# The last four adaLN vectors moved to the tensor engine, and longer pauses between the parts of the recurrences

## The chip, the cores and the metric

One Trainium2 chip, of which the kernel uses one core. The metric is the device time of one execution in microseconds (us); the figure for the kernel before is the median of three runs.

## The reference

One layer of an encoder trunk on `x` (1024 positions x 1024 channels) with a conditioning vector `c` (1024). Everything is float32.

```python
cond = silu(c)
mod = cond @ w_ada + b_ada                       # 1024 x 6144
sh1, sc1, gt1, sh2, sc2, gt2 = split(mod, 6)
h = rms_norm(x, g_pre_mix) * (1 + sc1) + sh1
u, v, rg_g, rg_x, ft_x = split(h @ w_in)         # 256, 256, 512, 512, 256 columns
y_gm = spatial_gating(gelu(u), gelu(v))
xr = centred_depthwise_conv(rg_x)
y_rg = bidirectional_rg_lru(xr) * gelu(rg_g)     # gates, then one scan per direction
y_ft = fourier_mix(ft_x)                         # real part of a 2-D DFT, then a linear map
y = concat(rms_norm(y_gm), rms_norm(y_rg), rms_norm(y_ft))
x = x + gt1 * rms_norm(y @ w_out, g_post_mix)
h = rms_norm(x, g_pre_ff) * (1 + sc2) + sh2
x = x + gt2 * rms_norm(square(relu(h @ w_ff1)) @ w_ff2, g_post_ff)
```

The change is about `mod`: `sh1` and `sc1` are needed at once, but `gt1`, `sh2`, `sc2` and `gt2` (the late vectors) only after the output projection `y @ w_out`.

## The kernel before

Channels lie on the partitions and positions along the free axis. `h` is kept in `HL` as a high and a low fp32r part; each large product is three fp32r matmuls (high by high, low by high, high by low: `mm3`, line 149). A 512-column matmul of this kind makes half of the positions of one 128-channel tile.

The part of the kernel around the change runs so:

- **zk**: the product of `h` with the 768 columns of `w_in` for the recurrence (tiles 0 to 3) and the Fourier group (tiles 4 and 5), first half of the positions for all, then the second half (line 672).
- **rg** (line 497), in a task `rg_all`: for each of four channel tiles a convolution (`conv`, DVE), two directions of gate matmuls (`gz`, 12 each), tanh, exp and square root on ACT, multiplications and a scan on DVE. The `yield`s in lines 526, 531 and 540 say how much matmul time shall pass before the next part is put into the program. The sum of the two directions is on POOL (line 541).
- **Fourier**: `ft_fold` (line 587) folds a tile by symmetry on POOL; `ft_a` (`fa`, `fx`) and `ft_b` (`fe`) are fp32 matmuls. `SEQ` (line 23) says in which order folds (f), first steps (a), second steps (b) and tiles of the remaining input projection (z) are written.
- **z tiles** 0, 1, 4, 5 (`z_full`), then `v_mm` (`vp`), then z tiles 6 and 7 in halves, with the layer norm of v, the spatial mixing (`rw`, `sp`) and three group norms (`gss`, `grs`, `dg`) between them, and then the output projection (`op`). From the start of `op` to the end, 741 us, the kernel computes what the change leaves alone.
- **ada** (line 452): for each of the 32 late blocks of 128 outputs, a 512 KB load of 128x1024 weights and one DVE instruction that multiplies by `cond`, which is spread over all partitions, and sums along the row. The task starts after the recurrences have ended (`join(trg)`, then `spawn(ada_all())`, line 710).

What sets the order: `mm` (line 142) adds each matmul's columns to a clock of the program; `pump` steps the tasks that are due by it. On each engine the instructions then stand in a fixed order and run strictly in that order. All loads are issued by SP, in order too. `load` takes one of four buffers of the tag "r", so a load waits until the last reader of the buffer's earlier content is done; the weights of `w_in`, `w_v`, `w_out` and the gates use the same four. For w_in and w_v the last reader is the instruction that makes the low part, on POOL (`WE`, line 171).

Of the kernel before, what the change touches and what calls it, by code (L numbers as in the profile page):

```python
# [7 lines left out]
F32 = mybir.dt.float32  # L8
# [11 lines left out]
PF = 7  # L20
CG = 8
RS = ((4.1, 2.0, 3.1, 2.1, 4.2), (3.1, 2.0, 2.6, 1.1, 3.7), (2.6, 2.0, 2.6, 0.6, 0.7))
SEQ = 'f0 f1 z02 a0 a1 b0 b1 z12 z42 z52'
WE = 'GGGGGGGG'
GD = ('VV VV VV VV', 'VV VV', 'V V V V')
FW = (3.5, 4.5, 1.5)
# [5 lines left out]
OEs = ('VV', 'VV', 'GG')  # L32
NG = (2.0, 5.0)
NR = ((4.5, 3.0), (8.0, 2.0))
ADY = (1.6, 32, 3)
RH = (2, 3)
D = 1024
S = 1024
# [5 lines left out]
_n = 0  # L44
for _name, _w in (("b_ada", 48), ("g_pre_mix", 8), ("g_post_mix", 8), ("g_pre_ff", 8), ("g_post_ff", 8),
                  ("g_mix_out", 8), ("conv_w", 16), ("conv_b", 4), ("b_a", 8), ("b_x", 8), ("lam", 8),
                  ("ft_b", 2), ("ln_g", 2), ("ln_b", 2)):
    PV[_name] = (_n, _w)
    _n += _w
NPV = _n  # L50


@with_exitstack
def trunk(ctx, tc, xT, c, pv, ident, w_ada, w_k, w_in, w_v, gates, k1, k2, k3, gmft, w_out, w_ff1, w_ff2, out):
    nc = tc.nc
    const = ctx.enter_context(tc.tile_pool(name="const", bufs=1))
    pool = ctx.enter_context(tc.tile_pool(name="pool", bufs=21))
# [19 lines left out]
    def ctile(name, n, dt=F32, bufs=1):  # L77
        return const.tile([128, n], dt, name=name, tag=name, bufs=bufs)
# [6 lines left out]
    ab = ctile("ab", 56)  # L85
    sp = ctile("sp", 64)

    ctile("pad0", 8)
    HL = const.tile([128, 8, 2, 1024], F32R, name="HL", tag="HL")
    big = const.tile([128, 8, 1024], F32, name="big", tag="big")  # L90
    ctile("pad1", 8)
    a1, b1, a2, b2, g1, g2, bp1 = (ab[:, i * 8:i * 8 + 8] for i in range(7))

    def col(name, i, n=1):
        a = PV[name][0] + i
        return pvt[:, a:a + n]
# [3 lines left out]
    clock = [0.0]  # L100
# [351 lines left out]
    def ada(blk):
        r = load(w_ada[blk], tag="r")
        V.scalar_tensor_tensor(out=r, in0=r, scalar=0.5, in1=cond, op0=MUL, op1=MUL,  # L454
                               accum_out=mod[:, blk:blk + 1])

    def vec(dst, blk, gname, one):
        V.tensor_tensor(out=dst, in0=mod[:, blk:blk + 8], in1=col("b_ada", blk, 8), op=ADD)
        if one:
            V.tensor_scalar(out=dst, in0=dst, scalar1=1.0, scalar2=None, op0=ADD)  # L460
        if gname:
            V.tensor_tensor(out=dst, in0=dst, in1=col(gname, 0, 8), op=MUL)

    def ada_all():
        for blk in range(16, 48):
            ada(blk)
            yield ADY[0] if blk < ADY[1] else ADY[2]
        vec(g1, 16, "g_post_mix", False)
        vec(b2, 24, None, False)
        vec(a2, 32, "g_pre_ff", True)  # L470
        vec(g2, 40, "g_post_ff", False)
# [25 lines left out]
    def rg(t):  # L497
        gs = gs_t.pop(t)
        xh, xl = xs_t.pop(t)
        xr = xr_t.pop(t)  # L500
        st = []
        for d in range(2):
            i = d * 4 + t
            ti, av = big[:, 2 + t, :] if d == 0 else tt("ti"), tt("av")
            pp = []
            for j in range(2):
                o = (d * 2 + j) * 128
                p = pa("gz")
                mm3(p, gs[:, o:o + 128], gs[:, 512 + o:640 + o],
                    [(xh[:, a:b], xl[:, a:b]) for a, b in HALF], True, True)  # L510
                pp.append(p)
                yield 0.1
            rr = [th("rr"), th("rr")] if t in RH else pp[0]
            for h, (a, b) in enumerate(HALF):
                A.activation(out=rr[h], in_=pp[0][h], func=AF.Tanh, scale=0.5, bias=bah[:, i:i + 1])
            for h, (a, b) in enumerate(HALF):
                A.activation(out=ti[:, a:b], in_=pp[1][h], func=AF.Tanh, scale=0.5, bias=bxh[:, i:i + 1])
            for h, (a, b) in enumerate(HALF):
                A.activation(out=av[:, a:b], in_=rr[h], func=AF.Exp, scale=m4[:, i:i + 1], bias=m4[:, i:i + 1])  # L519
            for h, (a, b) in enumerate(HALF):  # L520
                last = A.activation(out=rr[h], in_=rr[h], func=AF.Tanh, scale=p2[:, i:i + 1],
                                    bias=p2[:, i:i + 1])
            V.scalar_tensor_tensor(out=ti, in0=ti, scalar=1.0, in1=xr, op0=ADD, op1=MUL)
            V.scalar_tensor_tensor(out=ti, in0=av, scalar=1.0, in1=ti, op0=ADD, op1=MUL)
            st.append((rr, ti, av))
            yield 2.5
        with tc.issue_after(last.ins):
            for d in range(2):
                for h in range(2):
                    rgl[0] = A.activation(out=st[d][0][h], in_=st[d][0][h], func=AF.Sqrt, scale=0.25).ins  # L530
        yield 1.0
        for d in range(2):
            sq, ti, av = st[d]
            for h, (a, b) in enumerate(HALF):
                V.tensor_tensor(out=ti[:, a:b], in0=ti[:, a:b], in1=sq[h], op=MUL)
            if d == 0:
                V.tensor_tensor_scan(ti, av, ti, 0.0, op0=MUL, op1=ADD)  # L537
            else:
                V.tensor_tensor_scan(ti[:, ::-1], av[:, ::-1], ti[:, ::-1], 0.0, op0=MUL, op1=ADD)
            yield 1.2  # L540
        G.tensor_tensor(out=st[0][1], in0=st[0][1], in1=st[1][1], op=ADD)

    def norm_group(ks, n):
# [85 lines left out]

    def ft_b(t, at, ax):  # L630
        cosE = [kt[1][:, i * 257:i * 257 + 257] for i in range(3)]
        sinE = [kt[2][:, i * 257:i * 257 + 257] for i in range(2)]
        cosO = [kt[3][:, i * 256:i * 256 + 256] for i in range(2)]
        sinO = [kt[3][:, 512 + i * 256:768 + i * 256] for i in range(2)]
        ba = [at[:, j * 128:j * 128 + 128] for j in range(8)]
        ps = [pb("fe") for _ in range(4)]
        Ec, Es, Oc, Os = ps[0][:, 0:257], ps[1][:, 0:257], ps[2][:, 0:256], ps[3][:, 0:256]
        for dst, pairs in ((Es, ((ba[4], sinE[0]), (ba[5], sinE[1]))),
                           (Ec, ((ba[0], cosE[0]), (ba[1], cosE[1]), (ax, cosE[2]))),
                           (Os, ((ba[6], sinO[0]), (ba[7], sinO[1]))),  # L640
                           (Oc, ((ba[2], cosO[0]), (ba[3], cosO[1])))):
            for j, (w, x) in enumerate(pairs):
                mm(dst, w, x, j == 0, j == len(pairs) - 1)
            pump()
        y = big[:, 6 + t, :]
        b = col("ft_b", t)
        sn = [th("sn", F32, 257), th("sn", F32, 256)]
        A.copy(sn[0], Es)
        A.copy(sn[1], Os)
        Es, Os = sn  # L650
        V.scalar_tensor_tensor(out=y[:, 0:513:2], in0=Ec, scalar=b, in1=Es, op0=ADD, op1=SUB)
        V.scalar_tensor_tensor(out=y[:, 514:1024:2], in0=Ec[:, 255:0:-1], scalar=b, in1=Es[:, 255:0:-1], op0=ADD, op1=ADD)
        V.scalar_tensor_tensor(out=y[:, 1:512:2], in0=Oc, scalar=b, in1=Os, op0=ADD, op1=SUB)
        V.scalar_tensor_tensor(out=y[:, 513:1024:2], in0=Oc[:, ::-1], scalar=b, in1=Os[:, ::-1], op0=ADD, op1=ADD)

# [16 lines left out]
    for m in range(2, 6):  # L672
        p = {m: pb("zk")}
        for k in range(8):
            stage_mm(k, 1, p, (m,))
        evac_z(m, p, 1, V if m % 2 else A)
        if m == 2:
            kt[2] = load(k2, 770, "k2", "t")
            gm = load(gmft, 1024, "gm", "t")
        if m == 3:  # L680
            prep_to(1)
            for i, src, n in ((1, k1, 771), (3, k3, 1024)):
                kt[i] = load(src, n, "k%d" % i, "t")
# [23 lines left out]
            z_full(t, int(q[2]))  # L707
    kt.clear()
    join(trg)
    tad = spawn(ada_all(), 0.0)  # L710
    with tc.issue_after(rgl[0]):
        for t in range(2):
            A.activation(out=big[:, t, :], in_=big[:, t, :], func=AF.Gelu_apprx_tanh)
# [651 lines left out]
def _layout(inp):  # L1365
# [7 lines left out]
        cols(f("g_post_ff")[0]), cols(f("g_mix_out")[0]), cols(f("rg_conv_w")[0].reshape(-1)),  # L1373
        cols(f("rg_conv_b")[0]), cols(f("rg_b_a")[0].reshape(-1)), cols(f("rg_b_x")[0].reshape(-1)),
        cols(f("rg_lam")[0].reshape(-1)), cols(f("ft_b")[0].reshape(-1)), cols(f("gm_ln_g")[0]),
        cols(f("gm_ln_b")[0])], axis=1)
    w_in = f("w_in")[0]
    wi = w_in.reshape(8, 128, 14, 128).transpose(2, 1, 0, 3).reshape(14, 128, 1024)[:8]
    wv = w_in[:, 256:512].reshape(2, 4, 128, 256).transpose(0, 2, 1, 3).reshape(2, 128, 1024)
# [23 lines left out]
    for e in range(2):  # L1403
# [47 lines left out]
```

## Time and profile before

| | |
|---|---|
| median of three runs | 1030.87 us (1029.47 to 1032.01) |
| profiled execution | 1031.33 us, span 1029.5 us |
| PE busy | 963.3 us (94%) |
| DVE busy | 766.4 us (74%) |
| ACT busy | 501.0 us (49%) |
| POOL busy | 123.8 us (12%) |
| zk second half, rg, Fourier, first z tiles | about 90 to 214 us |
| vp, z tiles 6 and 7, norms | 214 to 288 us |
| op and feed-forward | 288 us to the end |

A time in the trace is counted from the start of the span. PE busy is the time in which a matmul was under way, at whichever clock; the granted clock (PEclk, 1.00 is full speed) stands beside it. Idle time of PE between two matmuls is put down to what the second one waited for.

### The profile page before, as it was taken

The page shows a single profiled execution, that of the slowest core. Times are in us where ns is not written, and L with a number is a line of the kernel's source. Part 1 is how long each engine was busy: PE and PEld are TensorE (multiplying, and loading weights), DVE is VectorE, ACT ScalarE, POOL GpSimd, SP SyncE. Part 2 cuts the span into 40 slices and gives each one's busy share as a digit, 9 for nine tenths or more (in the row PEclk, how much of TensorE's full clock was granted, in tenths as well). Part 3 has the DMA queues.
Part 4 walks back from the last instruction along what each step waited for, and adds up shares of the span by engine and source line. Part 5 has one row for each costly group of instructions (what it writes and reads, how often), then busy time and mean ns, then how long its engine had stood idle before and what let it go on. Part 6 is the DMA issues. An engine that isn't in the chain of part 4 may idle for free.

```text
span 1029.5 us, 13104 instructions
## 1 busy us (share of the span) xinstructions
PE 963.3 (94%) x4756; PEld 804.0 (78%) x4756; DVE 766.4 (74%) x1059; ACT 501.0 (49%) x764; POOL 123.8 (12%) x82
## 2 busy tenths in 40 slices
PE   6789975997899999999999999999999999999995
PEld 2568854896677997988888888888888888888995
DVE  6978888778897678897776776757665777688464
ACT  4454876622454355564544544545444455446311
POOL 4400391321140341000000000000000000000000
PEclk7989987998899999999999999999999999999998
DMA  9740200158235323054343343359899979987532
GB/s 343 286 142 21 82 24 18 62 202 288 102 131 177 129 97 113 32 183 185 132 179 138 133 191 126 123 198 331 297 392 341 362 269 335 328 277 258 187 133 93
DMA packets 80003, 191.59 MB, mean 186 GB/s; under 512 B 8769, under 2 KB 13121, under 8 KB 77890
## 3 DMA queue, kind: packets, MB, share of 16 engines
q1 hardware_dynamic: 76482, 186.56, 50.7%
q10 hardware_dynamic: 3456, 4.20, 1.1%
q8 instruction: 37, 0.61, 0.2%
q14 instruction: 28, 0.23, 0.1%
HBM read 144.58 MB, written 46.14 MB: 185 GB/s over the span
## 4 chain that ended last, share of the span: by engine, by line
PE 73%; DVE 14%; DMA 4%; ACT 4%; issue 3%; POOL 1%; SPq 0%; DVEq 0%; POOLq 0%
PE f L143 59%; PE op L143 6%; DMA raw<-in_w_ada_dram 3%; DVE raw L454 2%; PE z L143 2%; PE zk L143 2%; PE grs L143 1%; PE r L143 1%; DVE raw L291 1%; DVE HL L325 1%; DVE xr L481 1%; DVE big L537 1%; DMA big<-in_xT_dram 1%; ACT av L519 1%; DVE ss L279 1%
## 5 line engine op out<-in xcount | busy, mean ns | idle before, releaser
L143 PE MATMUL f<-x,x 128*128 128x512 f32 x768 | 236.2, 389 | 0.0
L143 PEld LDWEIGHTS f<-x,x 128*128 128x128 f32 x768 | 144.1, 188 | 29.8
L143 PE MATMUL f<-HL,wc 128*128 128x512 f32 x672 | 158.1, 390 | 0.0
L937 ACT CAST x<-R 128x1024 fp32r<-128x1024 f32 x96 | 100.3, 1053 | 110.8 <-DVE R L1131 56.0
L143 PE MATMUL f<-x 128*128 128x512 f32 x384 | 149.4, 389 | 0.0
L143 PEld LDWEIGHTS f<-HL,wc 128*128 128x128 f32 x672 | 125.0, 188 | 28.2 <-ACT big L1067 2.3
L948 DVE TENSOR_TENSOR x<-R,x 128x1024 fp32r<-128x1024 f32 x96 | 116.7, 1221 | 32.1 <-ACT x L937 30.7
L143 PE MATMUL f<-hc,wc 128*128 128x512 f32 x504 | 118.8, 389 | 0.0
L143 PEld LDWEIGHTS f<-hc,wc 128*128 128x128 f32 x504 | 94.6, 188 | 19.7
L143 PE MATMUL op<-HL,hi 128*128 128x256 f32 (+1 forms) x384 | 88.4, 324 | 0.0
L143 PEld LDWEIGHTS f<-x 128*128 128x128 f32 x384 | 72.1, 188 | 15.1
L143 PEld LDWEIGHTS op<-HL,hi 128*128 128x128 f32 x384 | 64.3, 190 | 6.5 <-issue 1.4
L1131 DVE TENSOR_TENSOR R<-R,o 128x512 f32<-128x512 f32 x64 | 43.6, 688 | 33.3 <-DMA o<-in_w_ff_dram 23.9
L143 PE MATMUL z<-HL,hi 128*128 128x512 f32 x192 | 63.3, 433 | 0.7 <-ACT ftg L614 0.7
L171 POOL TENSOR_TENSOR lo<-raw,hi 128x1024 fp32r<-128x1024 f32 x16 | 44.3, 2775 | 155.7 <-ACT hi L170 111.0
L143 PE MATMUL op<-HL,lo 128*128 128x256 f32 (+1 forms) x192 | 61.5, 320 | 0.0
L937 ACT CAST wc<-S 128x1024 fp32r<-128x1024 f32 x28 | 29.5, 1053 | 60.0 <-DVE S L1042 56.4
L454 DVE SCALAR_TENSOR_TENSOR raw<-raw,cond 128x1024 f32<-128x1024 f32 x32 | 48.5, 1521 | 13.4 <-DMA raw<-in_w_ada_dram 13.2
L948 DVE TENSOR_TENSOR wc<-S,wc 128x1024 fp32r<-128x1024 f32 x28 | 34.2, 1222 | 21.6 <-PE f L143 20.0
L143 PEld LDWEIGHTS z<-HL,hi 128*128 128x128 f32 x192 | 38.5, 204 | 11.9 <-issue 3.7
L143 PE MATMUL f<-HL,w 128*128 128x256 f32 x384 | 47.6, 285 | 0.0
L143 PEld LDWEIGHTS f<-HL,w 128*128 128x128 f32 x384 | 46.6, 192 | 0.6 <-issue 0.5
(298 smaller groups left out, 1637.8 us busy)
## 6 DMA issues: line engine op xcount, KB each, us to landing
raw<-in_w_ada_dram SPq DMA_DIRECT2D x48, 512.0 KB, 4.9
R<-Y SPq DMA_DIRECT2D x96, 256.0 KB, 4.8
R<-in_w_ff_dram SPq DMA_DIRECT2D x80, 256.0 KB, 5.0
raw<-in_w_ff_dram SPq DMA_DIRECT2D x32, 512.0 KB, 3.3
Y<-big SPq DMA_DIRECT2D x16, 1024.0 KB, 3.9
o<-in_w_ff_dram SPq DMA_DIRECT2D x64, 256.0 KB, 5.1
Y<-big SPq DMA_DIRECT2D x13, 768.0 KB, 3.4
SS<-R SPq DMA_DIRECT2D x32, 256.0 KB, 5.0
```

The lines of the kernel that those rows point to most:

```text
L143: pe[0] = T.matmul(o, w, x, start=start, stop=stop, skip_group_check=more).ins
L171: (eng or V).tensor_tensor(out=lo, in0=src, in1=hi, op=SUB)
L279: ssl[0] = eng.tensor_tensor(out=ss, in0=ss, in1=sq, op=ADD).ins
L291: V.scalar_tensor_tensor(out=r1, in0=r1, scalar=0.5, in1=cond, op0=MUL, op1=MUL, accum_out=mod[:, 8 + k:9 + k])
L325: V.scalar_tensor_tensor(out=HL[:, k, 1, a:b], in0=xk, scalar=b1[:, k:k + 1], in1=HL[:, k, 0, a:b], op0=ADD, op1=SUB)
L454: V.scalar_tensor_tensor(out=r, in0=r, scalar=0.5, in1=cond, op0=MUL, op1=MUL, accum_out=mod[:, blk:blk + 1])
L481: V.scalar_tensor_tensor(out=xr[:, o0:o1], in0=z[:, i0:i1], scalar=col("conv_w", k * 4 + t), in1=xr[:, o0:o1], op0=MUL, op1=ADD)
L519: A.activation(out=av[:, a:b], in_=rr[h], func=AF.Exp, scale=m4[:, i:i + 1], bias=m4[:, i:i + 1])
L537: V.tensor_tensor_scan(ti, av, ti, 0.0, op0=MUL, op1=ADD)
L937: order[0] = A.copy(dst, src).ins
L948: V.tensor_tensor(out=lo, in0=raw, in1=hi, op=SUB)
L1131: V.tensor_tensor(out=w, in0=w, in1=self.o, op=ADD if q == "M5" else SUB)
```

## The change

1. The four late vectors are computed on PE. For each vector and each of eight k-steps, a 512 KB load (`w_adn`, another layout of the same weights) and four fp32 matmuls `ad`: the weights operand is one column of silu(c) repeated 32 times, the four write to four groups of 32 partitions of one PSUM bank, 256 columns each. Then an ACT copy, two small matmuls that turn the rows into columns, and one to three tiny DVE operations. The program's clock counts one of the four matmuls. The 32 DVE instructions of line 454 are gone.
2. The task for them starts ahead of the last zk tile (m = 5), during the first recurrence, in place of after the last recurrence.
3. `SEQ` puts z tiles between the Fourier steps, and the `yield`s of the recurrences become 5.0, 2.0 and 2.5 from 2.5, 1.0 and 1.2.
4. `ft_b` uses two PSUM banks for four; two end columns go to ACT.
5. silu(c) is also made as a column, by three tiny operations at the start.

```diff
-SEQ = 'f0 f1 z02 a0 a1 b0 b1 z12 z42 z52'
+SEQ = 'f0 f1 z02 a0 z12 a1 b0 z42 b1 z52'
+RY = (5.0,2.0,2.5)
...
-ADY = (1.6, 32, 3)
+ADY = 2.0
...
+    cc = col("c", 0, 8)
+    ch = ctile("ch", 8)
+    A.activation(out=ch, in_=cc, func=AF.Tanh, scale=0.5)
+    V.tensor_scalar(out=ch, in0=ch, scalar1=0.5, scalar2=0.5, op0=MUL, op1=ADD)
+    V.tensor_tensor(out=cc, in0=cc, in1=ch, op=MUL)
...
     def ada_all():
-        for blk in range(16, 48):
-            ada(blk)
-            yield ADY[0] if blk < ADY[1] else ADY[2]
...
+        for v, (dst, gname, one) in enumerate(((b2, None, False), (a2, "g_pre_ff", True),
+                                               (g1, "g_post_mix", False), (g2, "g_post_ff", False))):
+            i = (1, 2, 0, 3)[v]
+            p = pb("ad")
+            for k in range(8):
+                r = load(w_adn[i, k], tag="r")
+                for g in range(4):
+                    mm(p[g * 32:g * 32 + 32, 0:256], cc[:, k:k + 1].to_broadcast([128, 32]), r[:, g * 256:g * 256 + 256],
+                       k == 0, k == 7, True)
+                clock[0] -= 3 * 4 * 256 / 2400.0
+                yield ADY
+            sb = th("adr", F32, 256)
+            A.copy(sb, p[:, 0:256])
+            yield 1.0
+            q = p[:, 256:264]
+            for j in range(2):
+                mm(q[:, j:8:2], sb[:, j * 128:j * 128 + 128], idt[:, 0:128:32], True, True)
+            V.tensor_tensor(out=dst, in0=q, in1=col("b_ada", 16 + 8 * i, 8), op=ADD)
...
-            yield 2.5
+            yield RY[0]
...
-        yield 1.0
+        yield RY[1]
...
-            yield 1.2
+            yield RY[2]
...
-        ps = [pb("fe") for _ in range(4)]
-        Ec, Es, Oc, Os = ps[0][:, 0:257], ps[1][:, 0:257], ps[2][:, 0:256], ps[3][:, 0:256]
+        ps = [pb("fe") for _ in range(2)]
+        Es, Ec, Os, Oc = ps[0][:, 0:255], ps[0][:, 255:512], ps[1][:, 0:256], ps[1][:, 256:512]
...
+        if m == 4:
+            tad = spawn(ada_all(), 0.0)
...
     join(trg)
-    tad = spawn(ada_all(), 0.0)
```

How the instructions move is seen at three places. The first is PE after the end of zk. Before, the gate matmuls of the third recurrence tile (`gz`) stand inside the first z tile, followed by the Fourier matmuls:

```order
L143 MATMUL z_942<-HL_72,hi_467 128x512 x2
L143 MATMUL z_942<-HL_72,lo_468 128x512
L143 MATMUL gz_987<-hi_875,gs_818 128x512
L143 MATMUL gz_988<-hi_875,gs_818 128x512
L143 MATMUL gz_987<-lo_876,gs_818 128x512
```

In the changed kernel the same z tile (z_891) holds ad groups, each one k-step of a late vector and each behind a load of its own:

```order
L144 MATMUL ad_808<-raw_962,pvt_64 32x256 x4
L144 MATMUL z_891<-HL_71,hi_470 128x512 x2
L144 MATMUL z_891<-HL_71,lo_471 128x512
L144 MATMUL z_891<-HL_71,hi_470 128x512 x2
L144 MATMUL z_891<-HL_71,lo_471 128x512
L144 MATMUL z_891<-HL_71,hi_470 128x512 x2
L144 MATMUL z_891<-HL_71,lo_471 128x512
L144 MATMUL ad_808<-raw_977,pvt_64 32x256 x4
L144 MATMUL z_891<-HL_71,hi_470 128x512 x2
L144 MATMUL z_891<-HL_71,lo_471 128x512
L144 MATMUL fa_987<-ftg_856,fo_867 128x128 x4
```

The gate matmuls in front of this piece are now those of the second recurrence tile, which before stood inside zk; further ad groups stand between the Fourier steps and inside z tiles 1, 4 and 5 and the start of vp.

The second place is SP, behind the load of the Fourier matrices. Before, the queue goes on to the weights of v and later z tiles:

```order
L164 DMA raw_1174<-in_w_in_dram 128x1024
L164 DMA k1_771<-in_k1_dram 128x771
L164 DMA k3_773<-in_k3_dram 128x1024
L164 DMA raw_1274<-in_w_v_dram 128x1024
L164 DMA raw_1333<-in_w_v_dram 128x1024
```

Now the loads of the late vectors stand there, among a few of the others:

```order
L165 DMA raw_892<-in_w_in_dram 128x1024
L165 DMA k1_741<-in_k1_dram 128x771
L165 DMA k3_743<-in_k3_dram 128x1024
L165 DMA raw_904<-in_w_adn_dram 128x1024
L165 DMA raw_919<-in_w_adn_dram 128x1024
L165 DMA graw_926<-in_gates_dram 128x512
L165 DMA raw_962<-in_w_adn_dram 128x1024
L165 DMA raw_977<-in_w_adn_dram 128x1024
L165 DMA raw_994<-in_w_adn_dram 128x1024
```

raw_977, which the seventh ad group reads, takes the buffer of raw_892; the reader that it waits for is the POOL instruction that makes lo_895.

The third place is POOL. Before, the end of the second fold is followed by the low part of that w_in tile, and the sum of the first recurrence tile stands ahead of both folds:

```order
L171 TENSOR_TENSOR lo_768<-raw_765,hi_767 128x1024
L541 TENSOR_TENSOR big_73<-big_73,ti_729 128x1024
L602 MEMSET ex_925 128x128
L602 MEMSET ex_939 128x128
L590 COPY pq_914<-big_73 128x2
```

In the changed kernel both folds come first (the first one directly behind the low part lo_738), and lo_895 and the sum follow their end:

```order
L616 COPY ex_874<-pq_863 128x1
L613 COPY fo_881<-pq_877 128x1
L615 MEMSET ex_888 128x128
L616 COPY ex_888<-pq_877 128x1
L172 TENSOR_TENSOR lo_895<-raw_892,hi_894 128x1024
L554 TENSOR_TENSOR big_72<-big_72,ti_756 128x1024
L172 TENSOR_TENSOR lo_1048<-raw_1045,hi_1047 128x1024
```

So the folds no longer wait behind the sum of the first recurrence tile, and lo_895 and all behind it wait for both folds.

## Rows read from the trace of the kernel before

**Rows 1.** The page, the chain that ended last by engine.

```profile
PE 73%; DVE 14%; DMA 4%; ACT 4%; issue 3%; POOL 1%; SPq 0%; DVEq 0%; POOLq 0%
```

**Rows 2.** Stretches: PE, PEld, DVE, ACT, POOL busy us; granted clock; DMA share; GB/s.

```profile
100.00:110.00 10.00, 10.00 (x45) 8.26 (x45) 9.58 (x10) 9.82 (x15) 0.00 (x0) 1.00 0.10 26
...
120.00:130.00 10.00, 9.32 (x45) 7.70 (x45) 10.00 (x7) 6.24 (x11) 6.96 (x6) 1.00 0.37 137
130.00:140.00 10.00, 6.36 (x20) 4.07 (x18) 8.90 (x7) 5.84 (x9) 10.00 (x10) 0.83 0.00 0
140.00:150.00 10.00, 7.38 (x38) 6.42 (x38) 8.12 (x8) 9.96 (x15) 10.00 (x10) 0.83 0.00 0
150.00:160.00 10.00, 6.27 (x34) 5.10 (x32) 9.96 (x6) 3.68 (x9) 4.44 (x2) 0.96 0.29 107
160.00:170.00 10.00, 3.56 (x10) 2.92 (x11) 6.38 (x9) 9.57 (x15) 0.00 (x0) 0.53 0.00 0
170.00:180.00 10.00, 7.91 (x28) 6.12 (x27) 9.89 (x8) 8.24 (x13) 3.83 (x2) 0.83 0.00 1
...
240.00:250.00 10.00, 7.74 (x38) 6.17 (x37) 6.99 (x18) 2.83 (x3) 2.40 (x1) 1.00 0.81 279
250.00:260.00 10.00, 5.60 (x25) 3.68 (x26) 9.14 (x22) 4.58 (x9) 0.00 (x0) 0.66 0.64 248
...
270.00:280.00 10.00, 5.58 (x24) 4.77 (x23) 7.58 (x12) 2.30 (x5) 2.36 (x1) 0.76 0.41 146
280.00:290.00 10.00, 10.00 (x41) 7.54 (x40) 7.85 (x11) 8.45 (x12) 4.71 (x2) 0.89 0.25 83
...
300.00:310.00 10.00, 8.16 (x39) 6.33 (x38) 9.70 (x14) 1.64 (x3) 2.65 (x1) 1.00 0.67 234
```

**Rows 3.** Waits of PE in 100 to 311 us: total, times, longest.

```profile
PE fe L143 <- ACT at L75: 9.6, 1, 9.6
PE grs L143 <- DVE dg L219: 8.2, 2, 6.7
```

**Rows 4.** The page, the group of the late vectors on DVE.

```profile
L454 DVE SCALAR_TENSOR_TENSOR raw<-raw,cond 128x1024 f32<-128x1024 f32 x32 | 48.5, 1521 | 13.4 <-DMA raw<-in_w_ada_dram 13.2
```

**Rows 5.** PE in time order: z tile 0 begins; fp32 matmuls at full and half width.

```profile
126.54 0.73 PE L143 MATMUL z<-HL,hi 128*128 128x512 f32 x2 [0.68 <-ACT ftg L614]
...
151.70 1.06 PE L143 MATMUL fa<-ftg,fo 128*128 128x128 f32 x8
152.59 0.39 PE L143 MATMUL fx<-ftg,ex 128*128 128x128 f32 x2
...
260.42 3.50 PE L143 MATMUL sp<-gm,vs 128*64 128x128 f32 x60
263.85 0.73 PE L143 MATMUL z<-HL,hi 128*128 128x512 f32 x2
```

**Rows 6.** POOL in time order: low parts and ops of both folds.

```profile
114.91 2.40 POOL L171 TENSOR_TENSOR lo<-raw,hi 128x1024 fp32r<-128x1024 f32 x1 [44.76 <-issue]
...
126.87 2.26 POOL L591 TENSOR_TENSOR pq<-big 128x511 f32<-128x511 f32 x1
...
140.61 1.26 POOL L592 TENSOR_TENSOR pq<-big 128x511 f32<-128x511 f32 x1
...
147.32 4.36 POOL L171 TENSOR_TENSOR lo<-raw,hi 128x1024 fp32r<-128x1024 f32 x1
```

**Rows 7.** ACT in time order: a Fourier tile's evacuation.

```profile
116.39 0.64 ACT L379 COPY big<-zk 128x512 f32<-128x512 f32 x1
```

**Rows 8.** Loads in 60 to 200 us: issues, KB, median us to landing.

```profile
raw<-in_w_in_dram SPq DMA_DIRECT2D x5, 512.0 KB, 3.8
...
raw<-in_w_v_dram SPq DMA_DIRECT2D x2, 512.0 KB, 3.2
```

**Rows 9.** PE in time order: z tile 6 and the output projection begin.

```profile
237.08 0.63 PE L143 MATMUL z<-HL,hi 128*128 128x512 f32 x2
...
288.06 0.72 PE L143 MATMUL op<-HL,hi 128*128 128x512 f32 x2
```

More of the change, by code (lines that the diff above doesn't have):

```diff
@@ L46 @@
                   ("g_mix_out", 8), ("conv_w", 16), ("conv_b", 4), ("b_a", 8), ("b_x", 8), ("lam", 8),
-                  ("ft_b", 2), ("ln_g", 2), ("ln_b", 2)):
+                  ("ft_b", 2), ("ln_g", 2), ("ln_b", 2), ("c", 8)):
     PV[_name] = (_n, _w)
@@ L53, in trunk @@
 @with_exitstack
-def trunk(ctx, tc, xT, c, pv, ident, w_ada, w_k, w_in, w_v, gates, k1, k2, k3, gmft, w_out, w_ff1, w_ff2, out):
+def trunk(ctx, tc, xT, c, pv, ident, w_ada, w_adn, w_k, w_in, w_v, gates, k1, k2, k3, gmft, w_out, w_ff1, w_ff2, out):
     nc = tc.nc
@@ L86, in trunk @@
     sp = ctile("sp", 64)
-    ctile("pad0", 8)
     HL = const.tile([128, 8, 2, 1024], F32R, name="HL", tag="HL")
     big = const.tile([128, 8, 1024], F32, name="big", tag="big")
-    ctile("pad1", 8)
+    ctile("pad", 16)
     a1, b1, a2, b2, g1, g2, bp1 = (ab[:, i * 8:i * 8 + 8] for i in range(7))
@@ L449, in trunk @@
     evac_z(1, ps, 1, V)
[L452 to L462, printed above, removed]
-    def ada_all():
-        for blk in range(16, 48):
-            ada(blk)
-            yield ADY[0] if blk < ADY[1] else ADY[2]
[L468 to L471, printed above, removed]
+    def ada_all():
+        for v, (dst, gname, one) in enumerate(((b2, None, False), (a2, "g_pre_ff", True),
[16 more added lines that the diff above has]
+            V.tensor_tensor(out=dst, in0=q, in1=col("b_ada", 16 + 8 * i, 8), op=ADD)
+            if one:
+                V.tensor_scalar(out=dst, in0=dst, scalar1=1.0, scalar2=None, op0=ADD)
+            if gname:
+                V.tensor_tensor(out=dst, in0=dst, in1=col(gname, 0, 8), op=MUL)
     xr_t, xs_t = {}, {}
@@ L631, in ft_b @@
         cosE = [kt[1][:, i * 257:i * 257 + 257] for i in range(3)]
-        sinE = [kt[2][:, i * 257:i * 257 + 257] for i in range(2)]
+        sinE = [kt[2][:, i * 257 + 1:i * 257 + 256] for i in range(2)]
         cosO = [kt[3][:, i * 256:i * 256 + 256] for i in range(2)]
@@ L646, in ft_b @@
         b = col("ft_b", t)
-        sn = [th("sn", F32, 257), th("sn", F32, 256)]
+        sn = [th("sn", F32, 255), th("sn", F32, 256)]
         A.copy(sn[0], Es)
@@ L650, in ft_b @@
         Es, Os = sn
-        V.scalar_tensor_tensor(out=y[:, 0:513:2], in0=Ec, scalar=b, in1=Es, op0=ADD, op1=SUB)
-        V.scalar_tensor_tensor(out=y[:, 514:1024:2], in0=Ec[:, 255:0:-1], scalar=b, in1=Es[:, 255:0:-1], op0=ADD, op1=ADD)
+        A.activation(out=y[:, 0:513:512], in_=Ec[:, 0:257:256], func=AF.Identity, bias=b)
+        V.scalar_tensor_tensor(out=y[:, 2:512:2], in0=Ec[:, 1:256], scalar=b, in1=Es, op0=ADD, op1=SUB)
+        V.scalar_tensor_tensor(out=y[:, 514:1024:2], in0=Ec[:, 255:0:-1], scalar=b, in1=Es[:, ::-1], op0=ADD, op1=ADD)
         V.scalar_tensor_tensor(out=y[:, 1:512:2], in0=Oc, scalar=b, in1=Os, op0=ADD, op1=SUB)
@@ L1375, in _layout @@
         cols(f("rg_lam")[0].reshape(-1)), cols(f("ft_b")[0].reshape(-1)), cols(f("gm_ln_g")[0]),
-        cols(f("gm_ln_b")[0])], axis=1)
+        cols(f("gm_ln_b")[0]), cols(f("c")[0])], axis=1)
     w_in = f("w_in")[0]
@@ L1414, in _layout @@
         "ident": np.eye(128, dtype=f32),
-        "w_ada": f("w_ada")[0].T.reshape(48, 128, 1024),
+        "w_ada": f("w_ada")[0][:, 0:2048].T.reshape(16, 128, 1024),
+        "w_adn": f("w_ada")[0][:, 2048:].reshape(8, 128, 4, 1024).transpose(2, 0, 1, 3),
         "w_k": w_in[:, 1024:].reshape(8, 128, 768),
```

## The prediction, made before the changed kernel ran

> **What bounds the kernel now.** First the chain that ended last [rows 1]: PE holds 73% of it, DVE 14% and DMA 4%. So most of the time is matmul time that no reordering removes, and the rest has to be looked for by stretches [rows 2]. Over most of the span PE is never idle; the idle time lies in two places. From 120 to 180 us PE is busy for 9.32, 6.36, 7.38, 6.27, 3.56 and 7.91 of 10 us, which leaves 19.2 us idle, and the granted clock falls to 0.53 to 0.96, which lengthens the busy time: busy time by missing clock is 1.1 + 1.3 + 0.3 + 1.7 + 1.3 = 5.6 us. Together 24.8 us. Those are the recurrences: PE has done its gate matmuls and waits for ACT and DVE; the longest wait is 9.6 us of `fe` for ACT [rows 3], because the z tiles stand behind `fe` in the fixed order. The second place is 240 to 310 us: idle 2.26 + 4.40 + 4.42 us in the stretches 240, 250 and 270, another 1.84 in 300, and low clock (0.66, 0.76, 0.89) worth 1.9 + 1.3 + 1.1 us. There `grs` waits 6.7 us for `dg` on DVE [rows 3]. DVE had nothing against making `dg`; it stood in order behind instructions of the late vectors, which take 48.5 us of DVE in all and made it wait 13.2 us for their loads [rows 4]. A change within 0.3% (3.1 us) can't be told from none here.
>
> **The change part by part.** I sum against the profiled execution, 1031.33 us, 0.46 above the median.
>
> *Taken back, first place.* With z tiles between the Fourier steps and ad groups everywhere, PE has other work at each place where it waited, as long as that work's own data are there. I take all 24.8 us as recovered; what speaks against that is the next but one part.
>
> *Added on PE.* Each of 32 k-steps has four fp32 matmuls of 256 columns and a quarter of the array's columns. No row shows that shape. Full-width fp32 matmuls follow each other after 0.111 us per record of 128 columns (0.89 us for eight `fa`), half-width ones, in two column groups, after 0.057 (3.43 us for sixty `sp`) [rows 5]. So two column groups run at once, each at the full-width pace. Four matmuls are eight records of 256 columns, 0.222 each alone: 0.44 us if all four groups run at once, 0.89 two at a time, 1.78 one by one; the change of shape costs little (0.1 us into `sp` and out of it each, from the same rows' ends), so 0.2 per k-step. That gives 0.69 (with 0.05 for the start), 1.1 and 2.0 us. I take 0.69, because two groups showed no loss at all: 32 x 0.69 = 22.1 us. The four turns into columns are two small fp32 matmuls each, at most two pairs of `fa` records and two changes, 0.6 us: 2.4. Together 24.5 us.
>
> The Trainium skill, page "TensorE: Matmul & The Clock Gate", section "The mechanism", says that a weight load overlaps a running matmul only when the row groups differ, and column groups share their rows. By that each of the eight records would wait for its own load, a k-step would take about 2 us (an estimate) and the sum would come to the 1058 us of rival C. The `sp` records don't agree with it for two groups, being 57 ns apart; no row shows four.
>
> *A new wait.* The seventh ad group needs raw_977, whose buffer is freed by lo_895 on POOL, behind both folds. When is PE there? In the trace of before, z tile 0 starts behind zk and `gp` at 126.54 after a wait of 0.68 [rows 5]. Now 24 gate matmuls of the second recurrence tile (0.222 each, 45 in 10 us [rows 2], 5.4 us) stand later and three ad groups (2.1) earlier, and the wait goes: about 122.5. Then come two ad groups, 12 gate matmuls, one ad group and most of z tile 0: 1.4 + 2.7 + 0.7 + 4.1, so 131.4 us. When is the load there? The folds can start when ACT has evacuated the Fourier tile, at 117 [rows 7], say 118. From the first large op at 126.9 to the low part at 147.3 the two folds took 20.4 us, the first beside a busy DVE (2.26 us for an op of 511 columns), the second partly alone (1.26) [rows 6]. All contended they would take some 24 us, all alone 14, by the ratio of these. DVE is busy until about 127 with the end of the first recurrence (an estimate from its order) and then itself waits behind POOL, so I take 18: 136. Then lo_895, 2.4 alone or 4.36 contended [rows 6], I take 3.3; the load, 3.2 to 3.8 [rows 8] and 0.4 of issue: 143. PE stands still from 131.4 to about 142.5: 11 us, between 6 (folds alone, shortest rows) and 18 (all contended). In order, it can't go on with z or `fa` behind it. The clock falls in such a gap as it did at 160 us; I add 1.2 us. What waits for PE there: ACT and DVE, for the gates of tile 1, second direction; so the recurrences end later, by this wait and the later start of the second one, some 16 us. That is hidden: nothing before the norms needs them, and these come after 249. Later ad loads wait for POOL too, but by the same counting some 8 us ahead of their groups, so they cost nothing unless POOL is that late.
>
> *Start of z tile 6.* 237.1 [rows 9] - 24.8 + 24.5 + 11 + 1.2 = 249.0 us, 12 later than before.
>
> *Taken back, second place.* From 237.1 to `op` at 288.1 [rows 9] PE needed 51.0 us, of which 11.1 idle and 4.3 low clock, so 35.6 of work. With the late vectors gone from DVE and SP by then, `dg` and the layer norm of v no longer stand behind loads. `op` begins at 249.0 + 35.6 = 284.6, 3.5 us earlier. The 1.84 us idle in 300 to 310, where DVE is still at 9.70 of 10 us with the last late vectors, go as well: 1.8. Behind that both kernels are alike.
>
> *Nothing.* The column of silu(c): three tiny operations while the first loads are on their way. `ft_b` with two banks: the same columns on PE, one small ACT operation more; ACT was busy for half the time. Loads: 16 MB as before, only earlier, at a time when the DMA share was 0 to 0.37. Longer `yield`s: order only.
>
> Sum: 1031.3 - 3.5 - 1.8 = **1026 us**.
>
> **The rivals.**
>
> *A: the wait for POOL is short.* If the folds run alone on their port (14 us) and the load takes 3.2, the wait is 6 and all ends at 1021. For it: DVE in its order waits for the folds' end itself from about 127. Against: POOL beside a busy DVE was slow at the first fold (2.26 us).
>
> *B: two column groups at once, not four.* The mechanism is the price of a k-step; the place is PE from 115 to 237 us. For the seven groups ahead of the wait nothing changes (PE comes later to a wait that ends at the same time). The 25 behind it cost 0.41 more each: 10 us, so 1036, **slower**. It decides from 0.21 us above my price on (5.3 / 25), that is 0.9 us per k-step. For it: only two were ever seen at once. Against: those two lost nothing.
>
> *C: one at a time* (or with weight loads in series). 25 x 1.3 = 32 us more: 1058. The rule of the page above would lead here. Against it is the 57 ns spacing.
>
> *D: the recovered idle time comes back.* Every recurrence still needs ACT, then DVE, then banks of PSUM; one bank is now held by `ad`, and a z tile in two banks waits for ACT copies that queue behind tanh and exp. If two rounds cost 2.5 us each, the time is 1031, no change. For it: ACT is busy for 9.96 and 9.57 of 10 us in two of the stretches [rows 2]. Against: `ft_b` gives two banks back.
>
> **How the numbers follow.** The forecast has 0.45; most of its spread (the wait between 6 and 18) lies below 1027.8, some within 0.3% of the median: 0.33 faster, 0.12 the same. A 0.16, faster. D 0.14: 0.10 the same, 0.04 slower. B 0.17 and C 0.08, slower. That makes 0.49 faster, 0.22 the same, 0.29 slower. The range goes from 1016 (A with 5 us more from the norms) to 1040 (B with some of D); C and the tails are left out. The likeliest case's own range is 1020 to 1033.
>
> **What would show it.** In the changed profile: `ad` groups 0.6 to 0.75 us from first record to the next matmul; an idle time of PE of 6 to 18 us ahead of an `ad` at about 131 us, put down to a load or to POOL; hardly any other idle time of PE until z tile 6, which begins near 249; `op` near 284.6. DVE without line 454 between 249 and 285. It would be wrong if `ad` groups take over 0.9 us, if the idle time before z tile 6 is spread over `gz` and z rows waiting for ACT, or if PE is idle for over 5 us again between z tile 6 and `op`.

## The result, and the profile after

The changed kernel takes 1054.49 us (median of four runs, 1053.27 to 1055.77) against 1030.61 us (median of four runs of the kernel before): a ratio of 1.0231, with a 95% interval of 1.0213 to 1.0250. It is slower by 24 us, where 1026 us and a gain were forecast. The profiled execution took 1053.27 us, with a span of 1051.4 us.

First the stretches. In the changed kernel (columns as in [rows 2]):

```profile
130.00:140.00 10.00, 3.66 (x25) 1.81 (x17) 6.54 (x4) 6.97 (x10) 7.11 (x12) 0.84 0.32 97
140.00:150.00 10.00, 9.12 (x49) 7.12 (x45) 8.49 (x8) 4.62 (x8) 1.21 (x1) 0.81 0.57 220
150.00:160.00 10.00, 9.00 (x42) 6.18 (x43) 6.16 (x6) 7.70 (x13) 2.40 (x1) 0.83 0.28 96
...
270.00:280.00 10.00, 4.40 (x19) 3.20 (x17) 10.00 (x5) 3.71 (x5) 10.00 (x5) 0.84 0.48 158
280.00:290.00 10.00, 6.28 (x23) 5.70 (x24) 5.58 (x6) 4.32 (x5) 4.88 (x2) 0.50 0.30 105
290.00:300.00 10.00, 7.78 (x23) 5.20 (x21) 4.98 (x8) 5.85 (x11) 0.00 (x0) 0.80 0.30 105
300.00:310.00 10.00, 5.69 (x18) 4.85 (x19) 9.58 (x16) 8.35 (x13) 0.00 (x0) 0.54 0.01 2
```

Where [rows 2] had 19.2 us of idle time in the stretches of the recurrences, 8.2 are left, most of it from 130 to 140 us; from 160 to 270 us PE is busy without a gap. But from 270 to 310 us it is idle for 15.9 us, at clocks of 0.50 to 0.84; from 270 to 300 us the low clock takes another 5.4 us (busy time by missing clock, as in the prediction). In 270 to 280 us DVE and POOL are both busy for the whole 10 us, with no more than five operations each. The waits of PE in 90 to 330 us (total, times, longest) name what was late:

```profile
PE grs L144 <- DVE gss L565: 15.9, 2, 9.3
PE ad L144 <- DMA raw<-in_w_adn_dram: 6.3, 1, 6.3
PE z L144 <- ACT ti L530: 1.3, 1, 1.3
PE gz L144 <- DVE ab L480: 0.5, 1, 0.5
```

And PE in time order, at the points of which the prediction spoke (start, us):

```profile
114.79 0.64 PE L144 MATMUL ad<-raw,pvt 128*32 128x256 f32 x8
115.36 2.13 PE L144 MATMUL zk<-HL,wkb 128*128 128x512 f32 x8
...
139.00 1.08 PE L144 MATMUL ad<-raw,pvt 128*32 128x256 f32 x8 [6.34 <-DMA raw<-in_w_adn_dram]
...
248.87 0.63 PE L144 MATMUL z<-HL,hi 128*128 128x512 f32 x2
...
283.73 1.87 PE L144 MATMUL grs<-ones,gss 128*128 128x1 f32 x8 [9.33 <-DVE gss L565]
...
304.31 1.84 PE L144 MATMUL grs<-ones,gss 128*128 128x1 f32 x8 [6.53 <-DVE gss L565]
306.01 1.20 PE L144 MATMUL op<-HL,hi 128*128 128x512 f32 x2
```

The three parts of the difference can be read against [rows 9]. Z tile 6 begins at 248.87 us, 11.8 later than before; the prediction had 249.0. From there to `op` it is 57.1 us, 6.2 more than the 51.0 of before, where 35.6 were forecast. From `op` to the end of the span it is 745.4 us, 4.0 more than before, where 1.8 less was forecast. Sum: 22.0, against 21.9 between the two spans (1051.4 and 1029.5).

What happens between 268 and 283 us, on DVE:

```profile
268.56 1.40 DVE L571 SCALAR_TENSOR_TENSOR big<-big,pvt,grs 128x512 f32<-128x512 f32 x2
...
271.40 3.42 DVE L809 TENSOR_TENSOR big<-big,sg 128x1024 f32<-128x1024 f32 x1
274.74 2.83 DVE L821 TENSOR_TENSOR gss<-gss,gsq 128x512 f32<-128x512 f32 x1
277.50 2.82 DVE L172 TENSOR_TENSOR HL<-big,HL 128x512 fp32r<-128x512 f32 x1
280.25 2.82 DVE L821 TENSOR_TENSOR gss<-gss,gsq 128x512 f32<-128x512 f32 x1
282.99 0.68 DVE L565 TENSOR_TENSOR gss<-gss,gsq 128x512 f32<-128x512 f32 x1
```

and on POOL:

```profile
267.85 14.68 POOL L172 TENSOR_TENSOR lo<-raw,hi 128x1024 fp32r<-128x1024 f32 x5 [18.05 <-DVE sg L787]
```

Five low parts of w_out run on POOL without a pause from 267.85 to 282.5 us. A DVE operation of 512 columns that takes 0.68 us when they are over takes 2.82 us beside them, about as long as one of theirs (14.68 / 5 = 2.9 us). PE waits at the end of this chain. The two operations at 268.56 us, whose input `grs` lies in PSUM, still take 0.70 us each although POOL is at work. The Trainium skill, page "SBUF — State Buffer", section "SBUF: two separate sides", has this as a rule: DVE operations with two SBUF inputs and POOL operations that read SBUF take one pair of ports in turn, each for its whole instruction. The trace agrees: from 271.40 us on one DVE operation ends per POOL operation, and those with one input in SBUF weren't slowed.

Why the five come together can be read from SP's rows. In the kernel before:

```profile
253.36 0.33 SPq L164 DMA_DIRECT2D raw<-in_w_out_dram  x1
260.52 0.33 SPq L164 DMA_DIRECT2D raw<-in_w_ada_dram  x1
267.55 4.29 SPq L164 DMA_DIRECT2D raw<-in_w_out_dram  x2
```

In the changed one, with ACT's rows for the high parts:

```profile
229.89 4.61 SPq L165 DMA_DIRECT2D raw<-in_w_out_dram  x4
247.47 2.68 SPq L165 DMA_DIRECT2D raw<-in_w_out_dram  x2
270.95 3.14 SPq L165 DMA_DIRECT2D raw<-in_w_out_dram  x2
...
266.68 1.03 ACT L171 CAST hi<-raw 128x1024 fp32r<-128x1024 f32 x1
269.21 2.93 ACT L171 CAST hi<-raw 128x1024 fp32r<-128x1024 f32 x3
```

Before, the loads of w_out stood among those of the late vectors and took turns with them for the four buffers; the third goes out at 253.36 us and the next two only at 267.55. With the late vectors gone from there, six are out by 250 us, four in a row and two more as soon as two buffers are free. Two of the six are split into parts by 250 us, so four tiles lie ready when ACT, in its fixed order, makes high parts again at 266.68 us, and their low parts follow each other on POOL; the load of the fifth goes out when the first is done. In the kernel before one tile was ready at that point (its high part is made at 263.96 us). The profile puts POOL's idle time ahead of the five down to DVE's `sg`, which ended at about the time of the first high part. All this is read from the rows; no run moved the loads alone.

The third part shows in the page's groups. In the changed kernel, matmuls that stream HL take longer and the others don't (last column but one: mean ns of one):

```profile
L144 PE MATMUL f<-HL,wc 128*128 128x512 f32 x672 | 161.7, 395 | 0.0
L144 PE MATMUL f<-hc,wc 128*128 128x512 f32 x504 | 119.4, 390 | 0.0
```

The kernel before had 390 and 389 there. The pace shows in time order; in the changed kernel three HL matmuls take 0.70 us,

```profile
250.27 0.63 PE L144 MATMUL z<-HL,hi 128*128 128x512 f32 x2
...
250.97 0.63 PE L144 MATMUL z<-HL,hi 128*128 128x512 f32 x2
```

and in the kernel before 0.68:

```profile
239.15 0.62 PE L143 MATMUL z<-HL,hi 128*128 128x512 f32 x2
...
239.83 0.39 PE L143 MATMUL z<-HL,hi 128*128 128x512 f32 x1
```

That is 233 ns for 227; those of the feed-forward that stream other tiles (`hc`, `x`) stay at 227. The diff has edits that the core shown above left out: to make room for eight columns of c it drops the 8-column pad ahead of HL, makes the one behind `big` 16 columns wide, for 8, and adds the 8-column tile `ch`. HL and `big` stay where they were; what is allocated behind them, the pool of large tiles with the weights in it, lies 16 float32 columns, 64 bytes per partition, higher.

The 4.0 us have other terms too, which nearly cancel. `op` begins behind the wait for `gss` at a low clock: 0.54 in the last stretch shown and 0.95 from 310 to 320 us, where the kernel before began it at 1.00. By missing clock that is some 2.3 us more. And the waits for `dg` and `gss` that the kernel before had behind the start of `op`, 1.9 us, are gone, as forecast.

### The profile page after: what moved, and what is told of

Same layout as the page of the kernel before. It is cut to its first block, busy times and chain, and to the rows that moved or that the text cites. A ratio compares the mean times of both kernels' runs of the same rounds, so it can differ in the third digit from the quotient of the medians.

```text
span 1051.4 us, 13590 instructions
## 1 busy us (share of the span) xinstructions
PE 992.8 (94%) x5028; PEld 805.9 (77%) x5028; DVE 720.6 (69%) x997; ACT 505.7 (48%) x773; POOL 116.1 (11%) x82
## 4 chain that ended last, share of the span: by engine, by line
PE 84%; DVE 7%; DMA 3%; issue 2%; POOL 2%; ACT 1%; SPq 0%; DVEq 0%; POOLq 0%; ACTq 0%
PE f L144 57%; PE op L144 7%; PE z L144 6%; PE zk L144 4%; PE vp L144 2%; PE gz L144 2%; PE ad L144 2%; PE grs L144 1%; PE r L144 1%; DMA wkr<-in_w_k_dram 1%; DMA raw<-in_w_ada_dram 1%; PE fe L144 1%; DMA xh<-in_xT_dram 1%; DVE HL L333 1%; DVE gss L821 1%
## 5 line engine op out<-in xcount | busy, mean ns | idle before, releaser
L144 PE MATMUL f<-HL,wc 128*128 128x512 f32 x672 | 161.7, 395 | 0.0
L144 PE MATMUL zk<-HL,wkb 128*128 128x512 f32 x192 | 48.4, 400 | 0.0
```

Of the source, the lines that this page charges most:

```text
L144: pe[0] = T.matmul(o, w, x, start=start, stop=stop, skip_group_check=more).ins
```

## The experiments

Three causes are proposed: the **place** of the pool, **POOL beside DVE** in the norms, and the **order** of the last sum of squares on DVE. The main rivals: that the recurrences, which end later, hold the norms back, and that the ad groups cost more than counted. The ratios that follow are against the kernel before on the same chip, with their 95% intervals.

**e1_place.** The pad goes, which puts the pool where it was before.

```diff
-    ctile("pad", 16)
+
```

> The changed kernel without its 16-column pad, so that the pool of large tiles lies 64 bytes lower per partition, where it lay before; the order of every engine is the same. Theory of the place: 512-column matmuls whose moving operand is HL go back from 233 to 227 ns apart, 1536 of them, and the 256-column ones from 118 back to 120; the stretch from op to the end is 741 to 742 us instead of 745.4, the total 1046 to 1050 us. Rival (the spacing comes from the ad groups, the weights' new layout or the chip): nothing changes, 1053 to 1055.

Measured: 1049.31 us, ratio 1.0173 (1.0157 to 1.0190), against 1.0231 of the changed kernel: 0.0058, or 6 us. From `op` (305.58) to the end of the span (1047.4) it is 741.8 us. The spacing is back at 227 ns, and the page's group with it:

```profile
L144 PE MATMUL f<-HL,wc 128*128 128x512 f32 x672 | 158.2, 391 | 0.0
```

The theory of the place holds; from `op` on it is worth 3.6 us (745.4 less 741.8). The waits of PE in the norms are unchanged (16.0 us in two).

**e3_before_shifted.** The same shift in the kernel before.

```diff
-    ctile("pad1", 8)
+    ctile("pad1", 24)
```

> The kernel before with its second pad 16 columns wider, so that the pool of large tiles lies 64 bytes higher per partition, where the changed kernel has it. Theory of the place: 512-column matmuls with HL as moving operand 233 ns apart, op to the end 745 us instead of 741.4, total 1035 to 1039. Rival (not the place): 1029 to 1032.

Measured: 1036.71 us, ratio 1.0049 (1.0031 to 1.0068). The page shows the same group at 394:

```profile
L143 PE MATMUL f<-HL,wc 128*128 128x512 f32 x672 | 161.7, 394 | 0.0
```

So 64 bytes cost 5 to 6 us in either kernel, with no instruction moved. What it is in the address that matters was not tried further.

**e2_low_on_act.** Takes POOL's part away without giving DVE anything.

```diff
-        (eng or V).tensor_tensor(out=lo, in0=src, in1=hi, op=SUB)
+        if eng is A:
+            A.copy(lo, src)
+        else:
+            (eng or V).tensor_tensor(out=lo, in0=src, in1=hi, op=SUB)
...
-        wlist.append((("out", k), w_out[k], G))
+        wlist.append((("out", k), w_out[k], A))
```

> The changed kernel, where the low parts of w_out are no longer subtracted on POOL but written by ACT as a plain copy (the low part's product is thus left out of the computation in its true form). Theory of POOL beside DVE: the DVE operations between 267 and 283 us take 0.7 to 1.2 us again instead of 2.8 to 3.4, PE's wait of 9.3 us for gss falls below 4, op starts 5 to 9 us earlier, total 1045 to 1049. Rival (the late recurrences or the order of DVE hold the norms back): PE waits for gss at least 8 us as before, total 1052 to 1056.

Measured: 1039.07 us, ratio 1.0073 (1.0055 to 1.0090): 0.0158 or 16 us under the changed kernel, more than expected. Z tile 6 to `op` falls from 57.1 to 43.5 us. PE's waits for gss fall from 15.9 to 5.4 us: the first, 9.3, to 0.4; the second, 6.5, to 5.0. So POOL is the cause of the first. The later end of the recurrences is not: their last sum on POOL stands at 226.53 us here, at 224.12 in the changed kernel and at 199.18 in the kernel before. The second has another cause for the most part.

**e5_low_on_dve.** The same with the true low parts, on DVE, on top of e1_place.

```diff
-        wlist.append((("out", k), w_out[k], G))
+        wlist.append((("out", k), w_out[k], V))
```

> The changed kernel with the pool of large tiles at its old place and the low parts of w_out subtracted on DVE instead of POOL (nothing left out). Theory of POOL beside DVE: eight operations of 1.2 us more on DVE, but none of 2.8 to 3.4 any more between z tile 6 and op; that stretch falls from 57 to 43 to 48 us, total 1035 to 1041. Rival (DVE's own work is the limit there): the stretch stays above 52 us, total over 1045.

Measured: 1035.86 us, ratio 1.0058 (1.0038 to 1.0078), 0.0115 or 12 us under e1_place. DVE has eight operations more and is done sooner; the operations that took 2.8 us in the changed kernel read:

```profile
269.73 0.69 DVE L821 TENSOR_TENSOR gss<-gss,gsq 128x512 f32<-128x512 f32 x1
270.33 0.68 DVE L172 TENSOR_TENSOR HL<-big,HL 128x512 fp32r<-128x512 f32 x1
```

From z tile 6 (246.53) to `op` (289.16) it is 42.6 us. What is left of PE's waits there is one of 5.9 us for gss.

**e11_order_on_after.** That second wait. In the changed kernel the last sum of squares of the small group (L565) stands on DVE behind the first norm of the recurrences (L827), whose first multiplication waits for PE:

```
L827 SCALAR_TENSOR_TENSOR big<-big,pvt,grs 128x512 x3
L172 TENSOR_TENSOR HL<-big,HL 128x512 x3
L827 SCALAR_TENSOR_TENSOR big<-big,pvt,grs 128x512
L571 SCALAR_TENSOR_TENSOR big<-big,pvt,grs 128x512 x2
L172 TENSOR_TENSOR HL<-big,HL 128x512
L565 TENSOR_TENSOR gss<-gss,gsq 128x512
```

In the kernel before the same sum (L552 there) stands directly ahead of the multiplications. The changed kernel alone with a longer pause ahead of them:

```diff
-NR = ((4.5, 3.0), (8.0, 2.0))
+NR = ((4.5, 5.5), (8.0, 2.0))
```

> The changed kernel with the second pause of the first recurrence norm 5.5 instead of 3.0, nothing else: the last sum of squares stands ahead of that norm's multiplications on DVE, while POOL still works beside DVE and the place is still the new one. Theory of the order: PE's second wait for gss, 6.5 us, falls below 2 and 4 to 8 us are won, total 1046 to 1051; the first wait of 9.3 us stays. Rival (POOL alone is the cause of both): within 2 us of 1054.5.

Measured: 1047.54 us, ratio 1.0153 (1.0132 to 1.0174), 0.0078 or 8 us under the changed kernel. PE's waits for gss:

```profile
PE grs L144 <- DVE gss L565: 11.5, 2, 9.3
```

The first stays at 9.3 and the second falls from 6.5 to 2.2. The order is a cause by itself.

**e6_in4_on_dve.** On top of e5_low_on_dve, the wait for the seventh ad load, which the prediction had named.

```diff
-WE = 'GGGGGGGG'
+WE = 'GGVGGGGG'
```

> As e5_low_on_dve, and the low part of w_in tile 4, for which the seventh ad load waits, is also on DVE, so that this load no longer stands behind both Fourier folds. Theory: PE's wait of 6.3 us ahead of an ad group near 132 us falls below 2, with its low clock 5 to 8 us are won, total 1029 to 1035. Rival (another wait takes its place, for the folds or for the recurrence's gates): less than 3 us are won.

Measured: 1033.56 us, ratio 1.0036 (1.0023 to 1.0050), and its interval overlaps that of e5. The wait is gone, and others stand in its place, 5.5 us in sum (such waits were 1.5 us in e5):

```profile
PE gz L144 <- DVE ab L480: 3.0, 1, 3.0
PE gz L144 <- ACT big L530: 1.5, 1, 1.5
PE gz L144 <- ACT big L708: 0.7, 1, 0.7
PE z L144 <- ACT ti L530: 0.3, 1, 0.3
```

Z tile 6 begins at 246.00 us against 246.53. The rival holds: PE reaches the recurrence's next gates sooner and waits for ACT and DVE there.

**e7_norm_order.** On top of e6, the order.

```diff
-NR = ((4.5, 3.0), (8.0, 2.0))
+NR = ((4.5, 4.5), (8.0, 2.0))
```

> As e6_in4_on_dve, with the second pause of the first recurrence norm 4.5 instead of 3.0 on the program's clock, which moves the last sum of squares of the small group's norm (gss) on DVE ahead of that norm's multiplications. Theory of the order: PE's second wait for gss, 5 to 6.5 us just ahead of op, falls below 2, total 3 to 6 us under that of e6. Rival (the wait is for the data, from ACT): within 2 us of e6.

Measured: 1024.81 us, ratio 0.9942 (0.9919 to 0.9965). It beats both kernels, by 6 us the one before; more was won than expected (0.0094 under e6, or 10 us). PE's only wait between z tile 6 (247.65) and `op` (284.88) is

```profile
PE grs L144 <- DVE gss L565: 0.5, 1, 0.5
```

and the stretch takes 37.2 us.

**e10_norm_only.** As e7, with the seventh ad load behind the folds again (`WE` as in the changed kernel).

> As e7_norm_order, but with the low part of w_in tile 4 back on POOL, so that PE's wait of 6.3 us for the seventh ad load is there again. If that wait is a cost of its own, 2 to 6 us slower than e7_norm_order (1024.8); if other waits take its place when it goes, within 2 us of it.

Measured: 1026.43 us, ratio 0.9951 (0.9935 to 0.9967). That can't be told from e7; PE's waits in 90 to 340 us are

```profile
PE ad L144 <- DMA raw<-in_w_adn_dram: 6.4, 1, 6.4
PE z L144 <- ACT ti L530: 1.3, 1, 1.3
```

and two under 0.6 us. So the wait of 6.3 us costs next to nothing that another would not take. Z tile 6 and `op` begin at

```profile
247.16 0.63 PE L144 MATMUL z<-HL,hi 128*128 128x512 f32 x2
...
282.81 0.70 PE L144 MATMUL op<-HL,hi 128*128 128x512 f32 x2
```

which is 35.7 us for the stretch, and from `op` to the end of the span (1022.4) it is 739.6 us.

**e4_order_alone.** The sequence and the pauses alone, in the kernel before.

```diff
-SEQ = 'f0 f1 z02 a0 a1 b0 b1 z12 z42 z52'
+SEQ = 'f0 f1 z02 a0 z12 a1 b0 z42 b1 z52'
...
-            yield 2.5
+            yield 5.0
...
-        yield 1.0
+        yield 2.0
...
-            yield 1.2
+            yield 2.5
```

> The kernel before with the new sequence of z tiles and Fourier steps and the longer waits of the recurrences alone; the late vectors stay on DVE behind the recurrences. If the idle time of 120 to 180 us is recovered by order alone, z tile 6 starts 8 to 15 us earlier than 237 and the total is 1018 to 1028; if the later end of the recurrences pushes the late vectors' loads into the norms, what is won is lost there and the total is 1028 to 1036.

Measured: 1029.07 us, ratio 0.9974 (0.9959 to 0.9990). In the profiled execution (1034.65 us, above the median of its runs) z tile 6 begins 15.3 us earlier than in [rows 9]:

```profile
221.74 0.63 PE L143 MATMUL z<-HL,hi 128*128 128x512 f32 x2
```

and nearly all of it is lost before `op`, which begins at 286.80, in waits for DVE, ACT and POOL:

```profile
PE grs L143 <- DVE gss L552: 9.6, 2, 7.7
PE grs L143 <- ACT gsq L551: 6.6, 1, 6.6
PE z L143 <- POOL lo L171: 5.3, 1, 5.3
```

The order alone does fill the recurrences. What takes it back isn't shown by a run of its own: the late vectors are still to come on DVE, and POOL and DVE lie side by side here too (three low parts on POOL from 224.26 us, and a late vector's operation beside them takes 3.39 us, 1.2 when POOL is idle).

**e8_ada_alone.** The late vectors on PE, with the sequence and the pauses of before.

```diff
-SEQ = 'f0 f1 z02 a0 z12 a1 b0 z42 b1 z52'
-RY = (5.0,2.0,2.5)
+SEQ = 'f0 f1 z02 a0 a1 b0 b1 z12 z42 z52'
+RY = (2.5,1.0,1.2)
```

> The changed kernel with the old sequence and the old, short waits of the recurrences: the late vectors on PE alone. If the ad groups by themselves fill PE's idle time in the recurrences, z tile 6 starts at 246 to 252 us as in the changed kernel (249) and the total is 1050 to 1057; if the order is what fills it, PE waits for ACT and DVE again between 130 and 180 us, z tile 6 starts at 256 or later and the total is 1058 to 1070.

Measured: 1061.61 us, ratio 1.0307 (1.0281 to 1.0333). Z tile 6 begins at 257.19 us, 8.3 later than in the changed kernel, and the wait for gss in the norms is there all the same:

```profile
PE grs L144 <- DVE gss L565: 15.8, 2, 9.3
PE ad L144 <- DMA raw<-in_w_adn_dram: 6.8, 4, 2.8
PE gp L144 <- DVE big L389: 4.8, 1, 4.8
```

So the loss in the norms comes with moving the late vectors, not with the order of the recurrences. That ad groups fill the gaps by themselves is not so. Where PE waits is not where it was expected, though: it is the ad loads and `gp`, and hardly ACT.

**e9_before_low_on_dve.** Whether the kernel before had the same to win from e5's edit.

```diff
-        wlist.append((("out", k), w_out[k], G))
+        wlist.append((("out", k), w_out[k], V))
```

> The kernel before with the low parts of w_out on DVE in place of POOL, nothing else. There the late vectors' loads spread these low parts, so that only one of them (at 272 us) lay beside an operation that PE waited for, and DVE is the busier engine. Theory: little changes, 1027 to 1033; the gain of the same edit in the changed kernel comes from the bunching that the change made. Rival (POOL beside DVE costs as much in the kernel before): under 1024, and the change itself is worth less than its comparison with this one.

Measured: 1032.79 us, ratio 1.0015 (0.9998 to 1.0032): no difference that can be measured. In the kernel before one low part on POOL (271.93 us) lies beside the chain that PE waits for, and makes a sum of squares take 2.82 us there (L552, 272.01 us). The wait for `gss` behind it falls from 4.4 to 2.1 us, and `op` begins at 286.10, 2 us sooner; but then it waits 4.0 us for a low part on DVE. So the same contention is there before, with 2 us to win and as much to lose; five in a row are the change's own. Whether the kernel before would gain from a longer pause in the norm was not tried.

Taken together, from the changed kernel's ratio of 1.0231: the place 0.0058, POOL beside DVE 0.0115, the order 0.0107 (e5 to e10). These three leave 0.9951, and without the ad load's wait 0.9942, which can't be told from it.

## Why the prediction was wrong

**The first half came out right, in part by luck.** Z tile 6 was put at 249.0 us and began at 248.87. That rests on errors that cancel: an ad group takes 0.57 us to the next matmul, not 0.69 (3.8 us less over 32); the wait for the seventh load was 6.34 us, at 139 us, not 11 (4.7 less: the second fold ran alone and lo_895 took 2.34 us). Against that the low clock of 130 to 160 us cost 3.9 us, not 1.2 (missing clock by busy time in the three stretches), and `gz` and `z` waited 1.8 us. The slower HL matmuls of the z tiles add 1.0 (168 by 6 ns). Some 3 us of it are not assigned. The wait itself came out as in rival A (6 us), and for its reason: the two folds took 15.6 us, not 18; yet z tile 6 did not begin earlier for it, and the time did not come out at A's 1021. The mechanism, a load behind both folds on POOL, is as predicted, but e6 and e10 show that it was worth next to nothing: the recurrence behind it has no slack to give.

**Rivals B and C fall.** All four column groups run at once: in the first group the eight records start at 0, 7, 14 and 20 ns and again from 240 ns, and 31 of the 32 groups take 0.57 us (the other, 1.01, follows the wait at 139 us, at a low clock). The rule of the Trainium skill on weight loads and row groups, page "TensorE: Matmul & The Clock Gate", section "The mechanism", that the prediction set against the change does not hold for column groups here. That C's 1058 us is near the measured 1054 is chance; nothing in the trace is of its kind. Rival D (waits in the recurrences) measured 1.8 us.

**The step that failed is "Taken back, second place".** It said that with the late vectors gone from DVE and SP, `dg` and the layer norm no longer stand behind loads, and took every idle time out: 35.6 us to `op`, where 57.1 were measured. Of the 21.5 us between, 15.9 are waits for `gss` and 5.4 the low clock in those stretches. The first part is true: no wait for `dg` is left. But the step did not ask what else had been held back by the late vectors' loads. They shared four buffers with the loads of w_out, and so had spread POOL's low parts (from the rows); without them five of these run side by side with the norms' chain on DVE and make each of its operations three to four times as long (e2, e5). And the order of that chain was moved by the change: the last sum of squares fell behind the multiplications (e11). The prediction had read the fold's contention on POOL from [rows 6] and used it for a wait in the first half; the same rows hold for any POOL operation beside a DVE chain that PE waits for. With both causes removed and the place restored, z tile 6 to `op` takes 35.7 us (e10) or 37.2 (e7), where 35.6 were forecast.

**"Behind that both kernels are alike" failed too.** From `op` on no instruction differs in kind, but the pool's place does, and it costs 3.6 us there (e1). The pads stood in the diff and were not weighed. The 1.8 us of idle time that the step took off did go, but the low clock at the start of `op` hid it; in e10, where `op` begins at full clock, it is 739.6 us from there to the end, and the prediction's figure is the same (741.4 less 1.8).

**What the prediction did see** is the gain itself: e10 takes 1026.4 us and e7 1024.8, where 1026 was forecast for a change that left the norms alone. That both halves must come together for it is likely, not shown: the order alone gives 0.9974 (e4), the late vectors alone were run only with the norms still held back (e8).

## What to carry to other kernels

When work is taken off an engine and a queue, ask what it had been holding back there: loads that share a ring of buffers throttle each other, and what is freed may start all at once, beside the chain that matters. Low parts on POOL and a serial chain of DVE operations with two inputs in SBUF should not run at the same time: here DVE did both sooner than the two engines side by side (1.2 us for a low part, against 2.8 for every operation of the chain). And before a change is judged by its time, put every large tile back to its old address: here that alone was 5 to 6 us.

## What the hardware showed that was not expected

- With nothing else changed, the address of the pool that holds the weights changes the pace of 512-column fp32r matmuls that stream HL: 227 ns where it lay before (the kernel before and e1), 233 with it 64 bytes higher (e3 and the changed kernel). Matmuls of 256 columns go the other way by some 2 ns (120 to 118).
- Four column groups of fp32 matmuls run at once: 256 columns by four groups, eight records, take 0.57 us to the next matmul, with the changes of shape into and out of them; the prediction's estimate without these changes was 0.44.
- A POOL subtraction of 1024 columns slows a DVE operation of 512 columns with both inputs in SBUF from 0.68 to 2.82 us, one for one; with one input in PSUM it stayed at 0.70.
